# Feed-forward products transposed by the DMA crossbar in two planes of 16-bit halves instead of by TensorE

## The chip, the cores and the metric

One core of one Trainium2 chip runs the whole program. The metric is device time in microseconds of one execution, from the first to the last instruction and what lies around them; lower is better. Engines: PE (TensorE), PEld (its weight loads), DVE (VectorE), ACT (ScalarE), POOL (GpSimd), SP (SyncE, which here only issues transfers).

## What is computed

A decoder of four layers over 256 rows of 1024 values. Each layer is a token mixer (differential attention, stick-breaking attention, sliding-window attention, then differential attention again) and a feed-forward part, each between two RMS norms. The change touches the feed-forward part alone:

```python
def swiglu(h, w_gate, w_up, w_down):
    return (jax.nn.silu(h @ w_gate) * (h @ w_up)) @ w_down

x = x + rms_norm(m, norm_gains[i, 1])
f = swiglu(rms_norm(x, norm_gains[i, 2]), ffn_w_gate[i], ffn_w_up[i], ffn_w_down[i])
x = x + rms_norm(f, norm_gains[i, 3])
```

`w_gate` and `w_up` are 1024 x 2816, `w_down` is 2816 x 1024, all float32.

## The kernel before, in words

The 256 rows are two **streams** of 128 rows (s = 0 and 1). Both run the same program and share the weights. A **unit** of weights is a tile of 128 x 1024 float32 that SP fetches into a stage buffer (`load_dma`, four stage buffers); ACT then copies it, rounded, to `hi`, and DVE subtracts to get `lo` (`split`). Eleven units of `hi` and `lo` are held (RING). Every product is three matmuls in fp32r: data high part by `hi`, data high part by `lo`, data low part by `hi`.

The feed-forward part (`ffn`) goes over 11 chunks of 256 hidden columns. For a chunk, `project` runs 24 matmuls of 512 columns into the PSUM bank `mm_f` (one bank for each stream), from four units: 256 columns of gate and 256 of up. Then ACT takes the tanh of half the gate (`t`), DVE makes `t = (t + 1) * gate` and `h = t * hsq * up`, both of 128 x 256. `h` has the rows on the partitions; the product with `w_down` needs it the other way round. So PE transposes `h` in two blocks of 128 x 128 into a PSUM bank (`th_f`), and `split_rows` makes the high part `hTh` (ACT) and the low part `hTl` (DVE) from it. `down(c)` multiplies these with two units of `w_down` into two PSUM banks that gather over all chunks (`acc_f`), 12 matmuls of 512 columns for each chunk and stream. In chunk c the code runs `project(c)`, the instructions on `t` and `h`, `down(c - 1)`, and then the transposes of chunk c and `split_rows`; so `hTh` and `hTl` of chunk c are first used after `project(c + 1)`. Stream 1 runs about one chunk behind stream 0.

What sets the order: an `Emitter` writes the two streams and the weight splits out in one sequence, by a clock of its own (a matmul column counts 1/2.4 ns, a transposed column four times that), and every engine runs its instructions in the order in which they were written. An instruction that waits holds up all that stand behind it on its engine. SP's queue is also in order: the weight fetches stand in it, each waiting until its stage buffer is free.

The names in the profile leave buffer numbers out; where an instruction is issued through the helper that records engine calls, its line is L181. In the orders shown below `f104` is layer 1, stream 0, chunk 4, and `f113` layer 1, stream 1, chunk 3.

Of the kernel before, what the change touches and what calls it, by code (L numbers as in the profile page):

```python
# [9 lines left out]
F32 = mybir.dt.float32  # L10
F32R = mybir.dt.float32r
BF16 = mybir.dt.bfloat16
I32 = mybir.dt.int32
AF = mybir.ActivationFunctionType
ALU = mybir.AluOpType
AX = mybir.AxisListType
# [2 lines left out]
P = 128  # L19
# [5 lines left out]
NCH = HIDDEN // 256  # L25
# [8 lines left out]
TMP = 8  # L34
# [123 lines left out]
def trunk_kernel(ctx, tc, x, positions, norm_gains, a_w_in, a_w_out, a_lambda, a_subln, b_w_in, b_w_out,  # L158
                 c_w_in, c_w_out, c_sinks, w_gate, w_up, w_down, out, depth=DEPTH):
    nc = tc.nc  # L160
# [3 lines left out]
    wk = ctx.enter_context(tc.tile_pool(name="wk", bufs=2))  # L164
# [3 lines left out]
    def bank(tag, s, shape, name):  # L168
        return ps.tile(shape, F32, tag=f"{tag}{s}", name=name, bufs=BANKS[tag])
# [16 lines left out]
    act, dve, pool, pe = (Start(e) for e in (nc.scalar, nc.vector, nc.gpsimd, nc.tensor))  # L186
# [66 lines left out]
    def split(u):  # L253
        t = staged.pop(u)
        hi = ringp.tile([P, 1024], F32R, tag="hi", name=f"hi_{u}")
        lo = ringp.tile([P, 1024], F32R, tag="lo", name=f"lo_{u}")
        act.activation(hi, t, AF.Copy)
        dve.tensor_tensor(lo, t, hi.bitcast(F32), ALU.subtract)
# [10 lines left out]

    pos_i = sm.tile([P, 2], I32, name="pos_i", bufs=1)  # L270
    nc.scalar.dma_start(pos_i, positions.rearrange("b (s p) -> p (b s)", p=P))
# [17 lines left out]
    pool.memset(quarter, math.pi / 2)  # L289
    act.activation(sm.tile([P, 1], F32, tag="preload", name="preload", bufs=1), quarter, AF.Sin)  # L290
    for j in range(32):
# [25 lines left out]
    def tables():  # L317
# [22 lines left out]
        yield  # L340
        act.activation(c, r, AF.Abs)
        rv = r.rearrange("p (s n) -> p s n", s=2)
        cv = c.rearrange("p (s n) -> p s n", s=2)
        for h in range(2):
            act.activation(cosf[:, :, 32 * h:32 * h + 32], cv, AF.Sin, bias=quarter, scale=-1.0)
        act.activation(sinf[:, :, 0:32], rv, AF.Sin, scale=-1.0)
        act.activation(sinf[:, :, 32:64], rv, AF.Sin)

# [24 lines left out]
    def mm(o, a, b, start, stop, f32=False):  # L373
        pe.matmul(o, a, b, start=start, stop=stop)
        n = 1
        for d in o.shape[1:]:
            n *= d
        em.t += n * COLUMN_NS * (4 if f32 else 1)
# [6 lines left out]
    def transpose(o, i):  # L385
        pe.transpose(o, i, ident)
        em.t += P * COLUMN_NS * 4
# [81 lines left out]
    def rows_product(acc, ah, al, w, first, last):  # L469

        cols = [slice(h * 512, (h + 1) * 512) for h in range(2)]
        if last:
            for h, cs in enumerate(cols):
                mm3(acc[h], ah, al, w[0][:, cs], w[1][:, cs], first, last)
        else:
            for v in range(2):
                for h, cs in enumerate(cols):
                    mm(acc[h], ah, w[v][:, cs], first and v == 0, False)
            for h, cs in enumerate(cols):
                mm(acc[h], al, w[0][:, cs], False, False)  # L480
# [14 lines left out]
    def project(s, xn, n, units_, name, first):  # L495

        b = bank("acc" if first else "mm", s, [P, n], f"mm_{name}")
        per = KT // units_
        for u in range(units_):
            w = yield ("w",)  # L500
            js = [(per * u + j, slice(j * n, (j + 1) * n)) for j in range(per)]
            for kt, cs in js:
                for v in range(2):
                    mm(b, xn[0][:, kt, :], w[v][:, cs], kt == 0 and v == 0, False)
            for kt, cs in js:
                mm(b, xn[1][:, kt, :], w[0][:, cs], False, kt == KT - 1)
        return b
# [40 lines left out]
    def score_products(s, sc, q, k, mask):  # L548
# [6 lines left out]
        for j in range(2):  # L555
            kbs = [kb for kb in range(s + 1) if mask(kb) is not None]
            for kb in kbs:
                mm(sc[j][:, :, kb * P:(kb + 1) * P], identb, mask(kb).unsqueeze(1).to_broadcast([P, 2, P]), False, kb == kbs[-1])

    def two_groups(s, name):  # L560
        return [[wk.tile([P, 4, P], F32R, tag=f"o{p}{s}", name=f"o{p}_{name}{g}") for p in "hl"] for g in range(2)]

    def split_rows(oT, sl, src, scale=None):

        hi, lo = oT[0][:, sl, :], oT[1][:, sl, :]
        if scale is None:
            act.activation(hi, src, AF.Copy)
            dve.tensor_tensor(lo, src, hi.bitcast(F32), ALU.subtract)
        else:
            act.activation(hi, src, AF.Copy, scale=scale)  # L570
            dve.scalar_tensor_tensor(lo, src, scale, hi.bitcast(F32), ALU.mult, ALU.subtract)

    def layer_a(s, i, xn):
        inst = i // 3
        name = f"a{i}{s}"
        nk = s + 1
        tabs = scaled_tables(s, xn[2], name)
        oT = two_groups(s, name)
        wT, st, qT = {}, {}, {}

# [99 lines left out]
    def layer_b(s, i, xn):  # L680
        name = f"b{i}{s}"
        nk = s + 1
        n = nk * P
        oT = two_groups(s, name)
        aT, qT = {}, {}

# [87 lines left out]
    def layer_c(s, i, xn):  # L774
        name = f"c{i}{s}"
        nk = s + 1
        n = nk * P
        tabs = scaled_tables(s, xn[2], name)
        oT = two_groups(s, name)

        def keys(chunk):
# [76 lines left out]
    def ffn(s, i, xn):  # L858
        name = f"f{i}{s}"
        half = sm.tile([P, 1], F32, tag=f"half{s}", name=f"half_{name}", bufs=1)  # L860
        hsq = sm.tile([P, 1], F32, tag=f"hsq{s}", name=f"hsq_{name}", bufs=1)
        dve.tensor_scalar(half, xn[2], 0.5, None, ALU.mult)
        dve.tensor_tensor(hsq, half, xn[2], ALU.mult)
        acc = None
        hT = {}

        def down(c):
            nonlocal acc
            for j in range(2):
                w = yield ("w",)  # L870
                if acc is None:
                    acc = [bank("acc", s, [P, 512], f"acc_{name}_{q}") for q in range(2)]
                j2 = 2 * (c % 2) + j
                rows_product(acc, hT[c][0][:, j2, :], hT[c][1][:, j2, :], w, c == 0 and j == 0, c == NCH - 1 and j == 1)
            del hT[c]

        for c in range(NCH):
            chunk = yield from project(s, xn, 512, 4, f"{name}{c}", c == 0)
            t = wk.tile([P, 256], F32, tag=f"as{s}", name=f"t_{name}{c}", bufs=STEPS)
            h = wk.tile([P, 256], F32, tag=f"as{s}", name=f"h_{name}{c}", bufs=STEPS)  # L880
            act.activation(t, chunk[:, 0:256], AF.Tanh, scale=half)
            dve.scalar_tensor_tensor(t, t, 1.0, chunk[:, 0:256], ALU.add, ALU.mult)
            dve.scalar_tensor_tensor(h, t, hsq, chunk[:, 256:512], ALU.mult, ALU.mult)
            if c == NCH - 1:
                yield from down(c - 2)
                yield from down(c - 1)
            elif c in (0, NCH - 2):
                yield ("d", 2200)
            else:
                yield from down(c - 1)  # L890
            tp = bank("tp", s, [P, 2, P], f"th_{name}{c}")
            for j in range(2):
                transpose(tp[:, j, :], h[:, j * P:(j + 1) * P])
            if c % 2 == 0:
                hT[c] = hT[c + 1] = [wk.tile([P, 4, P], F32R, tag=f"o{q}{s}", name=f"hT{q}_{name}{c}") for q in "hl"]
            split_rows(hT[c], slice(2 * (c % 2), 2 * (c % 2) + 2), tp)
        yield ("d", 700)
        yield from down(NCH - 1)
        return acc

    def stream(s):
        if s:
            yield ("d", 1500)
        for i in range(depth):
            kind = i % 3
            xn = pre_norm(s, 4 * i, f"n{i}{s}")
            yield ("d", 600)
            if i == 0 and s:
                scalars()
                act.on = dve.on = pool.on = pe.on = False  # L910
            gain = gain_of(i, 1)
            oT, name = yield from (layer_a, layer_b, layer_c)[kind](s, i, xn)
            acc = yield from out_proj(s, oT, name, (1, 1, 3)[kind])
            post_norm(s, acc, gain, f"m{i}{s}")
            yield ("d", 4000)
            gain = gain_of(i, 3)
            xn = pre_norm(s, 4 * i + 2, f"q{i}{s}")
            yield ("d", 600)
            acc = yield from ffn(s, i, xn)
            post_norm(s, acc, gain, f"e{i}{s}")  # L920
            if i < depth - 1:
                yield ("d", 4000)
        for h in range(2):
            cs = slice(h * 512, (h + 1) * 512)
            nc.sync.dma_start(out[0, s * P:(s + 1) * P, cs], xs[s][:, cs])
# [27 lines left out]
```

## Time and profile before

| what | value |
|---|---|
| median of 3 runs | 1204.88 us (1204.61 to 1205.26) |
| the profiled execution | 1205.73 us |
| its span, first to last instruction | 1203.9 us |
| granted TensorE clock, mean | 0.998 of 2.4 GHz |
| PE busy | 1185.8 us, 98% of the span |
| DVE, ACT, POOL busy | 779.2, 656.9, 48.1 us |
| DMA | 205.90 MB, mean 171 GB/s |

All durations of the rows come from the profiled execution, which took 0.85 us more than the median and 1.8 us more than its own span. Busy time is the union of an engine's instructions; matmuls overlap each other, so the time that a matmul costs PE is read from the distance of starts, not from its duration.

### The profile page before, as it was taken

To read this page: it belongs to the slowest core of one execution; us is meant where nothing else is said; L and a number is where in the kernel's file an instruction comes from. 1 tells how busy PE (TensorE), PEld (TensorE's weight loads), DVE (VectorE), ACT (ScalarE), POOL (GpSimd) and SP (SyncE) were. 2 spreads that over 40 slices of the span, in tenths; PEclk is the share of its full clock that TensorE was granted. 3 is DMA by queue.
4 is the path that set the end of the run, shared out by engine and by line. 5 is a ranking of instruction groups with operands and counts; after the bars stand their busy time and mean duration, and the time that the engine had idled before them with its cause. 6 is when DMAs were issued, how large, how long until landed. Compare 5 with 4: busy or idle time off the path is not lost.

```text
span 1203.9 us, 16738 instructions
## 1 busy us (share of the span) xinstructions
PE 1185.8 (98%) x6028; PEld 971.6 (81%) x6028; DVE 779.2 (65%) x1217; ACT 656.9 (55%) x1197; POOL 48.1 (4%) x141
## 2 busy tenths in 40 slices
PE   8999999999999999999999999999999999999997
PEld 7787888888878888888888778888888788888886
DVE  7876765555847666555588666655587776655553
ACT  5665644444756665444476655444475565544442
POOL 2000100000200000000000000000010001000000
PEclk9999999999999999999999999999999999999999
DMA  8635465565644546656664246555565453566550
GB/s 280 206 120 159 151 192 186 189 192 179 225 139 123 176 140 193 191 181 189 192 199 135 88 144 191 191 189 187 185 205 156 129 175 123 179 189 192 180 170 35
DMA packets 140838, 205.90 MB, mean 171 GB/s; under 512 B 9554, under 2 KB 104916, under 8 KB 140756
## 3 DMA queue, kind: packets, MB, share of 16 engines
q1 hardware_dynamic: 140048, 204.51, 54.0%
q8 instruction: 47, 0.77, 0.3%
q10 hardware_dynamic: 708, 0.34, 0.1%
q14 instruction: 35, 0.29, 0.1%
HBM read 203.76 MB, written 1.05 MB: 170 GB/s over the span
## 4 chain that ended last, share of the span: by engine, by line
PE 90%; DVE 3%; ACT 3%; issue 2%; POOL 1%; DMA 1%; ACTq 0%; DVEq 0%; POOLq 0%
PE mm_f L181 39%; PE acc_f L181 18%; PE acc_a L181 3%; PE mm_c L181 2%; PE acc_b L181 2%; PE sc_a L181 2%; PE th_f L181 2%; DVE lo L181 1%; PE acc_c L181 1%; PE sc_b L181 1%; DMA stage<-in_a_w_in_dram 1%; ACT hi L181 1%; PE pv_a L181 1%; PE sc_c L181 1%; PE pv_c L181 1%
## 5 line engine op out<-in xcount | busy, mean ns | idle before, releaser
L181 DVE TENSOR_TENSOR lo<-stage,hi 128x1024 fp32r<-128x1024 f32 x378 | 461.0, 1223 | 285.5 <-ACT hi L181 283.6
L181 ACT ACTIVATE hi<-stage 128x1024 fp32r<-128x1024 f32 x378 | 399.5, 1061 | 324.1 <-PE mm_f L181 154.4
L181 PE MATMUL mm_f<-hi,xh_q 128*128 128x512 f32 x704 | 280.2, 398 | 0.0
L181 PE MATMUL mm_f<-lo,xh_q 128*128 128x512 f32 x704 | 274.5, 390 | 0.0
L181 PE MATMUL mm_f<-hi,xl_q 128*128 128x512 f32 x704 | 217.4, 390 | 1.0 <-DVE xl_q L181 1.0
L181 PEld LDWEIGHTS mm_f<-hi,xl_q 128*128 128x128 f32 x704 | 132.2, 188 | 30.4 <-DVE xl_q L181 1.9
L181 PEld LDWEIGHTS mm_f<-hi,xh_q 128*128 128x128 f32 x704 | 132.2, 188 | 26.1 <-ACT xh_q L181 0.2
L181 PEld LDWEIGHTS mm_f<-lo,xh_q 128*128 128x128 f32 x704 | 132.4, 188 | 25.8
L181 PE MATMUL acc_f<-hi,hTh_f 128*128 128x512 f32 x352 | 113.7, 399 | 0.5 <-ACT hTh_f L181 0.5
L181 PE MATMUL acc_f<-hi,hTl_f 128*128 128x512 f32 x352 | 111.4, 392 | 0.5 <-DVE hTl_f L181 0.4
L181 PE MATMUL acc_f<-lo,hTh_f 128*128 128x512 f32 x352 | 110.7, 390 | 0.0
L181 ACT ACTIVATE t_f<-mm_f,half_f 128x256 f32<-128x256 f32 x88 | 41.7, 474 | 79.7 <-PE mm_f L181 79.7
L181 PEld LDWEIGHTS acc_f<-hi,hTl_f 128*128 128x128 f32 x352 | 65.9, 188 | 14.9 <-DVE hTl_f L181 1.0
L181 PEld LDWEIGHTS acc_f<-lo,hTh_f 128*128 128x128 f32 x352 | 66.1, 188 | 14.0
L181 PEld LDWEIGHTS acc_f<-hi,hTh_f 128*128 128x128 f32 x352 | 63.7, 188 | 11.9 <-ACT hTh_f L181 0.8
L181 DVE SCALAR_TENSOR_TENSOR t_f<-t_f,mm_f 128x256 f32<-128x256 f32 x88 | 36.7, 417 | 35.2 <-ACT t_f L181 35.1
L181 DVE SCALAR_TENSOR_TENSOR h_f<-t_f,hsq_f,mm_f 128x256 f32<-128x256 f32 x88 | 42.3, 480 | 2.7
L181 ACT ACTIVATE hTh_f<-th_f 128x256 fp32r<-128x256 f32 x88 | 33.0, 375 | 17.0 <-PE th_f L181 16.7
L181 DVE TENSOR_TENSOR hTl_f<-th_f,hTh_f 128x256 fp32r<-128x256 f32 x88 | 36.5, 418 | 5.6 <-ACT hTh_f L181 5.3
L181 ACT ACTIVATE e_a<-sc_a,nm_a 128x128 f32<-128x128 f32 (+1 forms) x64 | 26.0, 420 | 17.1 <-DVE nm_a L181 16.9
L181 PE MATMUL th_f<-ident,h_f 128*128 128x128 f32 x176 | 33.5, 271 | 0.0
L181 PEld LDWEIGHTS th_f<-ident,h_f 128*128 128x128 f32 x176 | 24.1, 139 | 11.4 <-DVE h_f L181 0.3
(584 smaller groups left out, 1543.1 us busy)
## 6 DMA issues: line engine op xcount, KB each, us to landing
stage<-in_ffn_w_gate_dram SPq DMA_DIRECT2D x176, 256.0 KB, 2.9
stage<-in_ffn_w_up_dram SPq DMA_DIRECT2D x176, 256.0 KB, 3.1
stage<-in_ffn_w_down_dram SPq DMA_DIRECT2D x88, 512.0 KB, 3.5
stage<-in_a_w_in_dram SPq DMA_DIRECT2D x48, 512.0 KB, 3.8
stage<-in_b_w_in_dram SPq DMA_DIRECT2D x24, 512.0 KB, 3.6
stage<-in_a_w_out_dram SPq DMA_DIRECT2D x16, 512.0 KB, 3.9
stage<-in_c_w_in_dram SPq DMA_DIRECT2D x10, 512.0 KB, 3.6
gain<-in_norm_gains_dram SPq DMA_DIRECT2D x8, 512.0 KB, 4.1
```

Of the source, the lines that this page charges most:

```text
L181: i = call(*args, **kw)
```

## The change

For chunks 0 to 9 of every layer and stream (10 x 2 x 4 = 80 of 88 tiles `h`), `h` is taken as 16-bit words. POOL copies it into two planes, low words and high words (`hp`, 128 x 512 of uint16). One DMA transpose on SP's queue turns the four blocks of 128 x 128 (`hq`). POOL copies them back, interleaved, into a float32 tile (`hx`). `split_rows` reads `hx` from SBUF where it read `th_f` from PSUM. Chunk 10 keeps the two TensorE transposes.

```diff
+    def turned_by_dma(h, name):
+        planes = wk.tile([P, 2, 256], U16, tag="t2k", name=f"hp_{name}", bufs=TMP)
+        pool.tensor_copy(planes, h.bitcast(U16).rearrange("p (n w) -> p w n", w=2))
+        tq = wk.tile([P, 4, P], U16, tag="t2k", name=f"hq_{name}", bufs=TMP)
+        nc.sync.dma_start_transpose(tq, planes.rearrange("p w n -> p (w n)"))
+        t = wk.tile([P, 2, P], F32, tag="t2k", name=f"hx_{name}", bufs=TMP)
+        pool.tensor_copy(t.bitcast(U16).rearrange("p b (t w) -> p w b t", w=2), tq.rearrange("p (w b) t -> p w b t", w=2))
+        return t
...
-            tp = bank("tp", s, [P, 2, P], f"th_{name}{c}")
-            for j in range(2):
-                transpose(tp[:, j, :], h[:, j * P:(j + 1) * P])
+            if c == NCH - 1:
+                t = bank("tp", s, [P, 2, P], f"th_{name}{c}")
+                for j in range(2):
+                    transpose(t[:, j, :], h[:, j * P:(j + 1) * P])
+            else:
+                t = turned_by_dma(h, f"{name}{c}")
...
-            split_rows(hT[c], slice(2 * (c % 2), 2 * (c % 2) + 2), tp)
+            split_rows(hT[c], slice(2 * (c % 2), 2 * (c % 2) + 2), t)
```

Orders of one round in layer 1, without and with the change. First ACT, from the tanh of stream 0's chunk 4 to that of its chunk 5. Before:

```order
L181 ACTIVATE t_f104_4776<-mm_f104_4692,half_f10_4161 128x256
L181 ACTIVATE hi_159_4802<-stage_159_4738 128x1024
L181 ACTIVATE t_f113_4812<-mm_f113_4731,half_f11_4371 128x256
L181 ACTIVATE hi_160_4833<-stage_160_4757 128x1024
L181 ACTIVATE hTh_f104_4826<-th_f104_4823 128x256
L181 ACTIVATE hi_161_4852<-stage_161_4781 128x1024
L181 ACTIVATE hi_162_4877<-stage_162_4800 128x1024
L181 ACTIVATE hTh_f112_4727<-th_f113_4862 128x256
L181 ACTIVATE hi_163_4896<-stage_163_4831 128x1024
L181 ACTIVATE hi_164_4920<-stage_164_4849 128x1024
L181 ACTIVATE t_f105_4912<-mm_f105_4830,half_f10_4161 128x256
```

With the change:

```order
L182 ACTIVATE t_f104_4857<-mm_f104_4770,half_f10_4221 128x256
L182 ACTIVATE hi_159_4883<-stage_159_4819 128x1024
L182 ACTIVATE t_f113_4893<-mm_f113_4812,half_f11_4434 128x256
L182 ACTIVATE hi_160_4917<-stage_160_4838 128x1024
L182 ACTIVATE hTh_f104_4910<-hx_f104_4908 128x256
L182 ACTIVATE hi_161_4936<-stage_161_4862 128x1024
L182 ACTIVATE hTh_f112_4808<-hx_f113_4950 128x256
L182 ACTIVATE hi_162_4964<-stage_162_4881 128x1024
L182 ACTIVATE hi_163_4983<-stage_163_4915 128x1024
L182 ACTIVATE hi_164_5007<-stage_164_4933 128x1024
L182 ACTIVATE t_f105_4999<-mm_f105_4914,half_f10_4221 128x256
```

Both high parts now read `hx`, and stream 1's stands one weight split earlier, so that three splits follow it instead of two.

DVE in the same round, from stream 1's low part to the first weight split after stream 0's `h` of chunk 5. Before:

```order
L181 TENSOR_TENSOR hTl_f112_4728<-th_f113_4862,hTh_f112_4727 128x256
L181 TENSOR_TENSOR lo_163_4897<-stage_163_4831,hi_163_4896 128x1024
L181 TENSOR_TENSOR lo_164_4921<-stage_164_4849,hi_164_4920 128x1024
L181 SCALAR_TENSOR_TENSOR t_f105_4912<-t_f105_4912,mm_f105_4830 128x256
L181 SCALAR_TENSOR_TENSOR h_f105_4913<-t_f105_4912,hsq_f10_4162,mm_f105_4830 128x256
L181 TENSOR_TENSOR lo_165_4939<-stage_165_4874,hi_165_4938 128x1024
```

With the change:

```order
L182 TENSOR_TENSOR hTl_f112_4809<-hx_f113_4950,hTh_f112_4808 128x256
L182 TENSOR_TENSOR lo_162_4965<-stage_162_4881,hi_162_4964 128x1024
L182 TENSOR_TENSOR lo_163_4984<-stage_163_4915,hi_163_4983 128x1024
L182 TENSOR_TENSOR lo_164_5008<-stage_164_4933,hi_164_5007 128x1024
L182 SCALAR_TENSOR_TENSOR t_f105_4999<-t_f105_4999,mm_f105_4914 128x256
L182 SCALAR_TENSOR_TENSOR h_f105_5000<-t_f105_4999,hsq_f10_4222,mm_f105_4914 128x256
L182 TENSOR_TENSOR lo_165_5026<-stage_165_4961,hi_165_5025 128x1024
```

Between stream 1's low part and stream 0's next `h` there are three weight subtractions instead of two.

SP's queue and POOL with the change, in the same round (before, POOL has nothing there, and SP's queue is the same without the transposes). SP:

```order
L251 DMA stage_161_4862<-in_ffn_w_gate_dram 128x2x256
L251 DMA stage_161_4862<-in_ffn_w_up_dram 128x2x256
L247 DMA stage_162_4881<-in_ffn_w_down_dram 128x1024
L566 DMA_TRANSPOSE hq_f104_4906<-hp_f104_4904 128x4x128
L247 DMA stage_163_4915<-in_ffn_w_down_dram 128x1024
L566 DMA_TRANSPOSE hq_f113_4948<-hp_f113_4946 128x4x128
L251 DMA stage_164_4933<-in_ffn_w_gate_dram 128x2x256
L251 DMA stage_164_4933<-in_ffn_w_up_dram 128x2x256
```

POOL:

```order
L182 COPY hp_f104_4904<-h_f104_4858 128x512
L182 COPY hx_f104_4908<-hq_f104_4906 128x2x256
L182 COPY hp_f113_4946<-h_f113_4894 128x512
L182 COPY hx_f113_4950<-hq_f113_4948 128x2x256
L182 COPY hp_f105_5046<-h_f105_5000 128x512
L182 COPY hx_f105_5050<-hq_f105_5048 128x2x256
```

Every transpose stands right behind a fetch of `w_down` and ahead of the fetch of a later unit. On POOL the copy back of one stream stands ahead of the copy out of the other.

## Rows read from the trace of the kernel before

**Rows 1.** The page of the profiled execution: the busy time of each engine (part 1), the granted TensorE clock by slice (part 2), and the chain that ended last by engine and by line (part 4).

```profile
PE 1185.8 (98%) x6028; PEld 971.6 (81%) x6028; DVE 779.2 (65%) x1217; ACT 656.9 (55%) x1197; POOL 48.1 (4%) x141
...
PEclk9999999999999999999999999999999999999999
...
PE 90%; DVE 3%; ACT 3%; issue 2%; POOL 1%; DMA 1%; ACTq 0%; DVEq 0%; POOLq 0%
PE mm_f L181 39%; PE acc_f L181 18%; PE acc_a L181 3%; PE mm_c L181 2%; PE acc_b L181 2%; PE sc_a L181 2%; PE th_f L181 2%; DVE lo L181 1%; PE acc_c L181 1%; PE sc_b L181 1%; DMA stage<-in_a_w_in_dram 1%; ACT hi L181 1%; PE pv_a L181 1%; PE sc_c L181 1%; PE pv_c L181 1%
```

**Rows 2.** The windows view of one stretch inside the feed-forward part of the first and of the last layer. Columns: busy us and number of instructions of each engine, granted clock, busy share of the DMA engines, GB/s.

```profile
170.00:270.00 100.00, 100.00 (x452) 82.19 (x451) 57.23 (x72) 46.79 (x60) 0.00 (x0) 1.00 0.60 186
...
1050.00:1150.00 100.00, 100.00 (x451) 82.19 (x450) 58.34 (x72) 46.46 (x60) 0.00 (x0) 1.00 0.60 188
```

**Rows 3.** The timeline of ACT, and below it of DVE, over one round of the two streams in the first layer's feed-forward part. Columns: start us, us, engine, line, operation, out<-in, count, and in brackets the idle time before it and what ended it.

```profile
264.31 0.47 ACT L181 ACTIVATE t_f<-mm_f,half_f 128x256 f32<-128x256 f32 x1 [0.30 <-PE mm_f L181]
...
269.97 0.39 ACT L181 ACTIVATE hTh_f<-th_f 128x256 fp32r<-128x256 f32 x1 [0.16 <-PE th_f L181]
...
275.07 0.36 ACT L181 ACTIVATE hTh_f<-th_f 128x256 fp32r<-128x256 f32 x1
...
281.18 0.47 ACT L181 ACTIVATE t_f<-mm_f,half_f 128x256 f32<-128x256 f32 x1 [0.30 <-PE mm_f L181]
...
265.64 0.48 DVE L181 SCALAR_TENSOR_TENSOR h_f<-t_f,hsq_f,mm_f 128x256 f32<-128x256 f32 x1
266.76 1.23 DVE L181 TENSOR_TENSOR lo<-stage,hi 128x1024 fp32r<-128x1024 f32 x1 [0.64 <-ACT hi L181]
...
269.36 0.48 DVE L181 SCALAR_TENSOR_TENSOR h_f<-t_f,hsq_f,mm_f 128x256 f32<-128x256 f32 x1
269.85 1.23 DVE L181 TENSOR_TENSOR lo<-stage,hi 128x1024 fp32r<-128x1024 f32 x1
```

**Rows 4.** The timeline of PE round the second pair of transposes in the same round (columns as in Rows 3).

```profile
273.45 0.62 PE L181 MATMUL acc_f<-hi,hTl_f 128*128 128x512 f32 x2
273.91 0.38 PE L181 MATMUL th_f<-ident,h_f 128*128 128x128 f32 x2
274.04 0.48 PE L181 MATMUL mm_f<-hi,xh_q 128*128 128x512 f32 x1
274.36 0.40 PE L181 MATMUL mm_f<-lo,xh_q 128*128 128x512 f32 x1
```

**Rows 5.** Groups of instructions by line, engine, operation and shape: busy us, mean ns of one | idle before, and what ended most of it.

```profile
L181 DVE TENSOR_TENSOR lo<-stage,hi 128x1024 fp32r<-128x1024 f32 x378 | 461.0, 1223 | 285.5 <-ACT hi L181 283.6
L181 ACT ACTIVATE hi<-stage 128x1024 fp32r<-128x1024 f32 x378 | 399.5, 1061 | 324.1 <-PE mm_f L181 154.4 <-PE acc_f L181 92.2 <-PE acc_a L181 15.7
...
L181 DVE SCALAR_TENSOR_TENSOR h_f<-t_f,hsq_f,mm_f 128x256 f32<-128x256 f32 x88 | 42.3, 480 | 2.7
...
L181 DVE SCALAR_TENSOR_TENSOR t_f<-t_f,mm_f 128x256 f32<-128x256 f32 x88 | 36.7, 417 | 35.2 <-ACT t_f L181 35.1
...
L181 PE MATMUL th_f<-ident,h_f 128*128 128x128 f32 x176 | 33.5, 271 | 0.0
L181 ACT ACTIVATE hTh_f<-th_f 128x256 fp32r<-128x256 f32 x88 | 33.0, 375 | 17.0 <-PE th_f L181 16.7
```

**Rows 6.** The waits view: engine and instruction <- what it waited for: us in total, times, longest us. The first is ACT's largest wait ahead of a weight split, the second its largest for a weight transfer.

```profile
ACT hi L181 <- PE mm_f L181: 154.4, 121, 1.7
...
ACT hi L181 <- DMA stage<-in_a_w_in_dram: 6.4, 8, 1.9
```

**Rows 7.** The groups of POOL (columns as in Rows 5).

```profile
L181 POOL TENSOR_SCALAR u_e<-ssp_e 128x1 f32<-128x1 f32 x8 | 2.4, 301 | 668.5 <-ACT junk_e L181 668.5
...
L181 POOL TENSOR_TENSOR lprod<-lam_in 128x256 f32<-128x256 f32 x1 | 0.7, 740 | 0.0
L181 POOL MEMSET reset<- 128x256 f32 x1 | 0.3, 311 | 0.0
...
L181 POOL CAST identb<-ident 128x128 bf16<-128x128 f32 x1 | 0.3, 289 | 0.1
...
L181 POOL MEMSET mask_causal<- 128x128 bf16 x1 | 0.2, 204 | 0.0
```

**Rows 8.** The timeline of DVE, and below it of POOL, at the end of the first layer (columns as in Rows 3).

```profile
314.50 0.47 DVE L181 SCALAR_TENSOR_TENSOR h_f<-t_f,hsq_f,mm_f 128x256 f32<-128x256 f32 x1
314.89 3.49 DVE L181 TENSOR_TENSOR lo<-stage,hi 128x1024 fp32r<-128x1024 f32 x3
318.30 0.42 DVE L181 TENSOR_TENSOR hTl_f<-th_f,hTh_f 128x256 fp32r<-128x256 f32 x1
...
314.91 3.55 POOL L181 TENSOR_SCALAR u_n<-ss_n 128x1 f32<-128x1 f32 x1 [3.38 <-ACT junk_n L181]
```

**Rows 9.** DMA issues: queue, operation, count, KB of one, median us from issue to landing.

```profile
stage<-in_ffn_w_gate_dram SPq DMA_DIRECT2D x176, 256.0 KB, 2.9
...
stage<-in_ffn_w_down_dram SPq DMA_DIRECT2D x88, 512.0 KB, 3.5
...
out_dram<-x SPq DMA_DIRECT2D x4, 256.0 KB, 2.1
...
lam_in<-in_a_lambda_dram ACTq DMA_DIRECT2D x1, 256.0 KB, 5.0
...
nsink<-in_c_sinks_dram ACTq DMA_DIRECT2D x1, 8.0 KB, 5.5
```

More of the change, by code (lines that the diff above doesn't have):

```diff
@@ L13 @@
 I32 = mybir.dt.int32
+U16 = mybir.dt.uint16
 AF = mybir.ActivationFunctionType
```

## Prediction

> **What bounds the kernel now.** I read the page first. PE is busy 98% of the span and holds 90% of the chain that ended last, at a clock that stands at 2.4 GHz in all 40 slices [rows 1]. The windows view says the same of the feed-forward part alone: PE has no idle time there, DVE is busy 57 to 58% and ACT 46 to 47% [rows 2]. So a microsecond taken off PE is a microsecond gained, as long as the other engines keep up. On the chain the transposes `th_f` have 2% [rows 1].
>
> Next the timeline. One **round** (one chunk of each stream) lasts 281.18 - 264.31 = 16.87 us, the distance of two tanh of stream 0 [rows 3]. Within it ACT takes up `hTh` at 269.97 and 275.07, while DVE had `h` ready at 266.12 and 269.84: 3.85 and 5.23 us later [rows 3]. That delay is free now, because PE works on other things meanwhile. ACT mostly waits for PE ahead of a weight split (154.4 us), since all eleven weight buffers are full, and hardly for a transfer (6.4 us, and that in the mixer) [rows 6].
>
> **Removed.** PE loses 80 pairs of transposes of the 88 (160 of 176 instructions, [rows 5]). What a pair costs is read from starts: two `acc_f` start at 273.45 and, 0.23 later, 273.68; without the pair the two matmuls after it would start at 273.91 and 274.14. The second one starts at 274.36 [rows 4]: 0.22 to 0.23 us for a pair, taken as 0.23. 80 x 0.23 = **18.4 us**, all of it on the path. A round bounded by PE would last 16.87 - 2 x 0.23 = 16.41 us. (The group's 33.5 us busy counts overlap with neighbours, so it is not the price.)
>
> **Added, the way of one tile.** From the end of `h` to the start of `hTh` there is now a chain with the length L:
> - copy out on POOL, 512 columns. No such copy is in the trace. Lower end: the cast of 128 columns takes 289 ns, and a further column costs 0.83 ns by the two memsets, (311 - 204) / 128 [rows 7]: 0.29 + 384 x 0.83 ns = 0.61 us. Upper end: `lprod`, two inputs, takes 740 ns for 256 columns [rows 7], so 1.48 us. One input is nearer the cast: I take 0.7.
> - transpose on SP, issue to landing, 128 KB. Lower end 2.1 us, the write of `x` out of SBUF. Upper end 5.5 us, `nsink`, the slowest landing. `lam_in`, 256 KB in short pieces, takes 5.0, and the 512 KB fetch on the same queue 3.5 [rows 9]. I take 3.6, the middle of 2.1 and 5.0, next to that fetch.
> - copy back on POOL, the same bounds; it writes every second word: 0.8.
> - four handovers of some 0.05 us: 0.2. In the rows `lo` starts within 0.1 us of its `hi`, and POOL within 0.1 of ACT.
>
> L = 0.7 + 3.6 + 0.8 + 0.2 = **5.3 us** (3.5 to 8.7 by the ends).
>
> **Where L lies on the path.** POOL runs copy out and copy back of stream 0, then those of stream 1; so the two L of a round follow each other. ACT has `hTh` of stream 1 in its queue ahead of three weight splits, and DVE has its three `lo` ahead of the `t` and `h` of stream 0's next chunk, which starts the next L (the orders shown with the change). This closes a loop: L, L, `hTh` 0.38, one `hi` 1.06, three `lo` 3 x 1.22 = 3.67, `t` 0.42, `h` 0.48 [rows 5], and 0.1 for handovers: 2L + 6.1. The other two splits and the tanh on ACT are done by then (0.38 + 3 x 1.06 + 0.47 = 4.03, before the last `lo` ends at 5.1).
>
> **The lock between DVE and POOL.** At 314.91 POOL starts an instruction `u_n` on one column; it takes 3.55 us and ends 0.08 after the third of three `lo` that DVE runs back to back from 314.89 to 318.38. The like of it, `u_e`, takes 0.30 [rows 7, 8]. So POOL cannot read beside a `lo`, which reads two tiles from SBUF, and gets no turn between two of them. In the changed order a `lo` stands right behind `h`, its `hi` is ready by then, and a `lo` starts within 0.02 us of the end of `h` (269.84 to 269.85, [rows 3]). So the copy out of stream 0 comes behind one `lo`: **1.2 us** more in each round. Stream 1's copy out starts when POOL comes free, while DVE waits for `hTh`: nothing. The Trainium skill (SBUF — State Buffer, section SBUF: two separate sides) states it as an exclusive lock between a VectorE instruction with two SBUF inputs and a GpSimd one that reads SBUF, held for the whole instruction by whichever starts first; the trace agrees with its 3.55 us. Were the copy first, DVE would wait instead.
>
> **The sum.** A round lasts 2 x 5.3 + 6.1 + 1.2 = 17.9 us, more than the 16.41 of PE, so the loop bounds it: +1.03 us against 16.87. There are 10 chunks x 4 layers = 40 rounds: +41 us. The profiled execution took 1205.7, so 1247; the median of the runs is 0.85 lower, so **1246 us**.
>
> **Costed at nothing.** SP's queue: each transpose holds back the fetches behind it until POOL has copied, and adds its own issue. The cover is the full weight buffers [rows 6]; ACT needs the unit behind stream 1's transpose only after that stream's `hTh` and two more splits, when a fetch (2.9 to 3.5 us, [rows 9]) has had the transpose, the copy back and 2.1 us. If that cover is gone, `hi` is late next, on the same loop. DMA engines: 60% busy in these stretches [rows 2], so a transpose may queue behind a fetch; that is inside 2.1 to 5.5. The split now reads SBUF, off PE's path. The buffers of the new tiles come round after 8 of them, over two tiles `h`. PE's idle time in a round is 17.9 - 16.4 = 1.5 us; no row shows the clock fall, so none is charged.
>
> **Rivals.**
> 1. *The crossbar is quick, PE stays the bound: faster.* The point is 2L + 7.3 = 16.87, L = 4.79, a transpose of 3.1 us with the copies as taken; below 2.9 nothing of the loop is seen. At the low ends, L = 3.5 gives 14.3, under 16.41, and the time is 1205.7 - 18.4 = 1187 us. For it speak the 2.1 and 2.9 us of plain transfers of twice the bytes; against it, that a transpose moves 2-byte words and stands behind a 512 KB fetch in SP's queue. If the lock alone does not bite, the round is 16.7 and the time 1199. The Trainium skill (Advanced Engine Details and Errata, section X-Bar Transpose (TRN2)) says that such transposes are as fast as regular transfers; no row here shows one, and by that rule this rival wins.
> 2. *The crossbar is slow.* At the 5.0 of `lam_in`, L = 6.7, the round is 20.7 and the time 1205.7 + 3.83 x 40 = 1359 us; at all the upper ends (L = 8.7, round 24.7) it is 1519. For it speaks that short pieces land latest [rows 9]; against it, that those two landed on another queue at the start. The Trainium skill (VectorE: DVE Perf Modes, section The three transpose paths) gives 1309 ns for one 128 x 128 block through the crossbar against 390 on TensorE, and advises TensorE where the result may go to PSUM, as here; no run here shows it. As an estimate by that page, four blocks one after another are 5.2 us, which would be this rival. Within it lies a clock that falls because PE idles (every round would then need twice PE's 16.4); 0.02.
> 3. *Even.* A loop within 0.06 us of the old round.
>
> That the transposes are not replaced can be left out: PE has 80 pairs fewer in its order.
>
> **How the numbers follow.** About 0.2% (2.4 us) is what a measurement of this kernel can tell from no change. The forecast, 1208 to 1300 us (a transpose of 3.1 to 4.3 us with the copies as taken), has 0.47. Rival 1 has 0.23, rival 3 0.05, rival 2 (over 1300) 0.25, about half of it over 1370. The range goes from the floor of PE, 1186, to 1370, which a transpose of 5.1 us gives. Cases of both signs lie in it; the forecast's own range is 1208 to 1300. Faster 0.23, same 0.05, slower 0.72.
>
> **What would show it.** Right: rounds of 17 to 20 us by the distance of stream 0's tanh; `hTh` on ACT waiting for POOL, 80 times; `hp` stretched by about 1.2 us in one stream; PE idle some 1.5 us in a round. Each term has its row: copies 0.7 and 0.8, landing 3.6. Wrong: PE without idle time and rounds of 16.4 (rival 1), or landings over 4.5 us (rival 2), or waits of `hi` for a fetch, which would make SP's queue the cause.

## The result and the profile after

Before 1204.89 us in the median of four runs (1204.61 to 1205.26); after **1190.55 us** (1187.64 to 1192.48). The profiled run of the changed kernel took 1192.19 us, with a span of 1190.4. The change makes the kernel faster, by 1.2%: ratio 0.9879, interval [0.986, 0.9897]. The four runs after lie 4.8 us apart, those before 0.7; that spread is part of what has to be explained. From here, lines of the changed kernel are one higher than before (L182 for L181).

The page of the changed kernel: busy times, the chain that ended last, groups (busy us, mean ns of one | idle before, and what ended it) and DMA issues (KB, median us from issue to landing).

```profile
PE 1168.0 (98%) x5868; PEld 958.5 (81%) x5868; DVE 779.4 (65%) x1217; ACT 649.0 (55%) x1197; POOL 175.0 (15%) x301
...
PE 68%; DMA 10%; DVE 7%; POOL 5%; ACT 5%; issue 4%; SPq 0%; POOLq 0%; ACTq 0%; DVEq 0%
...
L182 ACT ACTIVATE hTh_f<-hx_f 128x256 fp32r<-128x256 f32 x80 | 33.4, 418 | 229.4 <-POOL hx_f L182 229.4
...
L182 POOL COPY hp_f<-h_f 128x512 uint16<-128x512 uint16 x80 | 70.4, 880 | 301.5 <-DVE h_f L182 273.0
...
L182 POOL COPY hx_f<-hq_f 128x512 uint16<-128x512 uint16 x80 | 62.8, 785 | 254.8 <-DMA hq_f<-hp_f 252.5
...
stage<-in_ffn_w_gate_dram SPq DMA_DIRECT2D x176, 256.0 KB, 3.1
...
stage<-in_ffn_w_down_dram SPq DMA_DIRECT2D x88, 512.0 KB, 4.5
...
hq_f<-hp_f SPq DMA_TRANSPOSE x80, 2.5
```

Against [rows 1] the share of PE in the chain fell from 90% to 68%, that of DMA rose from 1 to 10% and that of POOL from 1 to 5%: the loop that the prediction described exists, and PE is no longer the only bound. `hTh` waits for the copy back all 80 times, 229.4 us. The median landing is 2.5 us from issue, and the fetches land later than in [rows 9] (3.1 for 2.9, 4.5 for 3.5).

The windows view, one stretch of the first and one of the last layer:

```profile
170.00:270.00 100.00, 100.00 (x443) 82.81 (x442) 57.52 (x72) 45.25 (x61) 21.77 (x26) 1.00 0.77 210
...
1050.00:1150.00 100.00, 97.33 (x420) 79.14 (x419) 57.08 (x72) 45.16 (x60) 20.99 (x24) 0.98 0.72 202
```

PE has no idle time in the first stretch, as in [rows 2], but 2.67 us in the second. By the distance of stream 0's tanh a round lasts 16.3 us where PE bounds it: in layers 1 and 2 all six rounds that begin with chunks 3 to 8 of stream 0. In layer 0 single rounds take 16.5 to 17.2, in layer 3 16.7 to 18.1. Two tanh of stream 0 in layer 1, then two in layer 3:

```profile
526.09 0.47 ACT L182 ACTIVATE t_f<-mm_f,half_f 128x256 f32<-128x256 f32 x1 [0.30 <-PE mm_f L182]
542.41 0.47 ACT L182 ACTIVATE t_f<-mm_f,half_f 128x256 f32<-128x256 f32 x1 [0.30 <-PE mm_f L182]
```

```profile
1091.65 0.45 ACT L182 ACTIVATE t_f<-mm_f,half_f 128x256 f32<-128x256 f32 x1
1109.78 0.45 ACT L182 ACTIVATE t_f<-mm_f,half_f 128x256 f32<-128x256 f32 x1
```

In layer 1 the tanh waits for PE and the round is 16.32 us; in layer 3 it waits for nothing but its place in ACT's order, and the round is 18.13. A late round does not always cost what it is late: in layer 0 shorter ones, down to 15.3 us, follow, and the stretch from the first tanh to the last takes 173.99 us, against 173.44 in the kernel without transposes (first experiment). In layer 3 it takes 178.82 against 173.44. So the gain is the predicted floor of PE, less what the late rounds cost, which in the profiled execution is nearly all in layer 3.

POOL's timeline over the latest round, in layer 3, shows the loop whole (start us, us, what, and in brackets the idle time before and what ended it):

```profile
1094.38 1.45 POOL L182 COPY hp_f<-h_f 128x512 uint16<-128x512 uint16 x1 [5.93 <-DVE h_f L182]
1101.93 0.76 POOL L182 COPY hx_f<-hq_f 128x512 uint16<-128x512 uint16 x1 [6.10 <-DMA hq_f<-hp_f]
1102.60 0.61 POOL L182 COPY hp_f<-h_f 128x512 uint16<-128x512 uint16 x1
1105.82 0.77 POOL L182 COPY hx_f<-hq_f 128x512 uint16<-128x512 uint16 x1 [2.60 <-DMA hq_f<-hp_f]
1112.51 1.45 POOL L182 COPY hp_f<-h_f 128x512 uint16<-128x512 uint16 x1 [5.93 <-ACT t_f L182]
```

Copy out and back of stream 0, copy out and back of stream 1, then 5.93 us in which ACT and DVE do the splits, the tanh and the next `h`. The 5.93 recurs to 0.02 us in every round of layers 0 and 3 that begins with chunks 2 to 8, as read from POOL's timeline there. (In the sums of the loop, here and below, the landing of a turn is POOL's idle time between copy out and copy back.) With 1.45 for the first copy, 0.76, 0.61, 2.56 for the usual landing of stream 1, 0.76 and 5.93, less 0.08 by which the records overlap, the loop is **12.0 us + landing of stream 0**. The landings of layer 0 and 3 check it: 4.67 gave a round of 16.68, 5.21 gave 17.20, 6.10 gave 18.13. By this sum a round is over PE's 16.3 when that landing is over 4.3 us. In the 12 rounds of layers 0 and 3 that begin with chunks 3 to 8, all of them set by the loop, the landings of stream 0 run from 3.34 to 6.10, median 4.2: the loop stands at the balance with PE. Six of these rounds are late: four have a landing of stream 0 over 4.3, and in the other two, of 16.5 and 17.5 us, stream 1's landing took 3.12 and 4.15.

DVE beside the first of these rows, in the same kernel, shows why that copy takes 1.45 us and not 0.61:

```profile
1093.74 0.48 DVE L182 SCALAR_TENSOR_TENSOR h_f<-t_f,hsq_f,mm_f 128x256 f32<-128x256 f32 x1
1094.14 1.22 DVE L182 TENSOR_TENSOR lo<-stage,hi 128x1024 fp32r<-128x1024 f32 x1
```

The copy starts 0.24 us into a `lo` and ends 0.47 after it. In layers 1 and 2 this `lo` comes later, because its `hi` waits there for PE to free a weight buffer, and the copy takes 0.61. With that and landings of 4.2 us in the median (3.56 to 4.76) the same sum is 15.3 us in these layers, and PE sets the round.

### The profile page after: what moved, and what is told of

Same layout as the page of the kernel before. It is cut to its first block, busy times and chain, and to the rows that moved or that the text cites. A ratio compares the mean times of both kernels' runs of the same rounds, so it can differ in the third digit from the quotient of the medians.

```text
span 1190.4 us, 16818 instructions
## 1 busy us (share of the span) xinstructions
PE 1168.0 (98%) x5868; PEld 958.5 (81%) x5868; DVE 779.4 (65%) x1217; ACT 649.0 (55%) x1197; POOL 175.0 (15%) x301
## 4 chain that ended last, share of the span: by engine, by line
PE 68%; DMA 10%; DVE 7%; POOL 5%; ACT 5%; issue 4%; SPq 0%; POOLq 0%; ACTq 0%; DVEq 0%
PE mm_f L182 26%; PE acc_f L182 12%; DMA hq_f<-hp_f 8%; DVE lo L182 4%; PE acc_a L182 3%; POOL hp_f L182 3%; ACT hi L182 2%; PE mm_c L182 2%; PE acc_b L182 2%; PE sc_a L182 2%; POOL hx_f L182 1%; PE acc_c L182 1%; DMA stage<-in_a_w_in_dram 1%; PE sc_b L182 1%; PE pv_a L182 1%
## 5 line engine op out<-in xcount | busy, mean ns | idle before, releaser
L182 DVE TENSOR_TENSOR lo<-stage,hi 128x1024 fp32r<-128x1024 f32 x378 | 457.6, 1224 | 130.3 <-ACT hi L182 127.6
L182 ACT ACTIVATE hi<-stage 128x1024 fp32r<-128x1024 f32 x378 | 393.8, 1056 | 124.9 <-PE mm_f L182 49.9
L182 PE MATMUL mm_f<-hi,xh_q 128*128 128x512 f32 x704 | 275.8, 392 | 2.3 <-DVE h_f L182 2.3
L182 PE MATMUL mm_f<-lo,xh_q 128*128 128x512 f32 x704 | 274.8, 390 | 0.0
L182 PE MATMUL mm_f<-hi,xl_q 128*128 128x512 f32 x704 | 217.5, 390 | 1.0 <-DVE xl_q L182 1.0
L182 ACT ACTIVATE hTh_f<-hx_f 128x256 fp32r<-128x256 f32 x80 | 33.4, 418 | 229.4 <-POOL hx_f L182 229.4
L182 PEld LDWEIGHTS mm_f<-hi,xh_q 128*128 128x128 f32 x704 | 132.6, 188 | 30.9 <-ACT t_f L182 2.4
L182 PEld LDWEIGHTS mm_f<-hi,xl_q 128*128 128x128 f32 x704 | 132.4, 188 | 29.5 <-DVE xl_q L182 1.8
L182 PEld LDWEIGHTS mm_f<-lo,xh_q 128*128 128x128 f32 x704 | 132.6, 188 | 27.4 <-DVE lo L182 0.2
L182 DVE TENSOR_TENSOR hTl_f<-hx_f,hTh_f 128x256 fp32r<-128x256 f32 x80 | 34.0, 425 | 162.9 <-ACT hTh_f L182 162.9
L182 POOL COPY hp_f<-h_f 128x512 uint16<-128x512 uint16 x80 | 70.4, 880 | 301.5 <-DVE h_f L182 273.0
L182 PE MATMUL acc_f<-hi,hTh_f 128*128 128x512 f32 x352 | 111.3, 392 | 0.5 <-ACT hTh_f L182 0.5
L182 PE MATMUL acc_f<-lo,hTh_f 128*128 128x512 f32 x352 | 110.6, 390 | 0.7 <-DVE lo L182 0.5
L182 PE MATMUL acc_f<-hi,hTl_f 128*128 128x512 f32 x352 | 111.0, 391 | 0.0
L182 POOL COPY hx_f<-hq_f 128x512 uint16<-128x512 uint16 x80 | 62.8, 785 | 254.8 <-DMA hq_f<-hp_f 252.5
L182 PEld LDWEIGHTS acc_f<-lo,hTh_f 128*128 128x128 f32 x352 | 65.9, 188 | 15.2 <-DVE lo L182 1.5
L182 PEld LDWEIGHTS acc_f<-hi,hTh_f 128*128 128x128 f32 x352 | 65.7, 188 | 14.3 <-ACT hTh_f L182 0.8
L182 PEld LDWEIGHTS acc_f<-hi,hTl_f 128*128 128x128 f32 x352 | 65.8, 188 | 14.0 <-DVE hTl_f L182 0.5
L182 ACT ACTIVATE t_f<-mm_f,half_f 128x256 f32<-128x256 f32 x88 | 41.3, 469 | 59.6 <-PE mm_f L182 59.3
L182 DVE SCALAR_TENSOR_TENSOR t_f<-t_f,mm_f 128x256 f32<-128x256 f32 x88 | 36.6, 416 | 20.5 <-ACT t_f L182 20.4
L182 DVE SCALAR_TENSOR_TENSOR h_f<-t_f,hsq_f,mm_f 128x256 f32<-128x256 f32 x88 | 42.3, 480 | 2.9
L182 ACT ACTIVATE e_a<-sc_a,nm_a 128x128 f32<-128x128 f32 (+1 forms) x64 | 26.0, 420 | 17.0 <-DVE nm_a L182 16.9
```

The costliest lines, as they stand in the source:

```text
L182: i = call(*args, **kw)
```

## Experiments

The kernel before ran beside them at 1205.7 us (first four), 1205.2 (the next three) and 1205.15 (the last).

### The floor: no transposes at all

In place of the transposes `h` itself is handed to the split; the transposes of ten chunks are left out.

```
-                t = turned_by_dma(h, f"{name}{c}")
+                t = h.rearrange("p (b t) -> p b t", b=2)
```

> Leaves the transposes of chunks 0 to 9 out altogether: the split reads h as it is (the products with w_down then use an h that is not turned). No hp, hq, hx; PE's order is that of the changed kernel. Theory (PE is the bound, the way through the crossbar is nearly hidden): the floor of the prediction, 1204.9 - 80 x 0.23 = 1186.5 us, rounds of 16.3 to 16.4 us in all four layers, and a spread of the runs as small as before (under 1 us); the 4 us by which the changed kernel lies above that are late transposes. Rival (the gain or the rest comes from the changed order, not from the transposes): about 1190.5 with the same uneven rounds in layers 0 and 3.

Measured: 1185.17 us (1184.95 to 1185.64), ratio 0.9831 [0.9817, 0.9844], rounds of 16.3 in all layers. The floor holds; the changed kernel stands 5.4 us above it (6.2 when each is set against the kernel before that ran beside it). The windows give the share of the DMA engines without the transposes:

```profile
170.00:270.00 100.00, 100.00 (x443) 82.81 (x442) 59.66 (x73) 48.15 (x61) 0.00 (x0) 1.00 0.62 194
```

0.62, against 0.77 after: some 13 transposes in 100 us take 15% of all 16 engines, although they move 1.7 MB beside 19. The page counts their packets, first in the changed kernel, then in this one:

```profile
DMA packets 184361, 216.42 MB, mean 182 GB/s; under 512 B 53074, under 2 KB 148436, under 8 KB 184276
```

```profile
DMA packets 140837, 205.88 MB, mean 174 GB/s; under 512 B 9555, under 2 KB 104917, under 8 KB 140757
```

That is 544 more small packets for each of the 80 transposes, of some 240 bytes.

### The transposes on ScalarE's queue

```
-        nc.sync.dma_start_transpose(tq, planes.rearrange("p w n -> p (w n)"))
+        nc.scalar.dma_start_transpose(tq, planes.rearrange("p w n -> p (w n)"))
```

> The DMA transposes are issued from ACT's queue instead of SP's. Theory (the landings over 2.5 us, up to 6, come from standing behind weight fetches in SP's queue): all 80 landings near 2.5 us, rounds of 16.3 us in all layers, 1187 to 1188 us. Rival (the DMA engines are shared, whichever queue a transfer stands in): landings from 2.5 to 6 us as now, 1190 to 1192 us. Against both: ACT now issues 1.2 us for each transpose and waits for POOL ahead of stream 1's tanh; if that binds, rounds are longer everywhere and the time is over 1195.

Measured: 1274.85 us (1272.53 to 1275.07), ratio 1.057 [1.0555, 1.0584]. The landings did not become shorter: from chunk 3 on stream 0's transposes took 4.9 to 7.3 us, the median of all is 3.7. So it isn't the place in SP's queue that delays them. What goes with a late landing, on either queue, is the fetches under way: in the changed kernel's trace, of the 71 transposes whose landing is recorded, the 50 issued with at most 512 KB of fetches not yet landed took 2.4 us in the median, the 21 issued with more (768 KB or 1 MB) took 4.0; here the 31 with more, up to 1.5 MB, took 5.3. And ACT, in order, now stands behind each transpose's copy out and its issue of 1.2 us (waits view):

```profile
ACT hi L182 <- issue: 57.9, 32, 3.1
ACT t_f L182 <- issue: 45.8, 11, 4.7
```

### Each transpose twice

The first of the two writes a tile that nobody reads.

```
+        nc.sync.dma_start_transpose(wk.tile([P, 4, P], U16, tag="t2k", name=f"hd_{name}", bufs=TMP), planes.rearrange("p w n -> p (w n)"))
         nc.sync.dma_start_transpose(tq, planes.rearrange("p w n -> p (w n)"))
```

> Every DMA transpose is issued twice in a row from SP's queue, the first into a tile that nobody reads; the copy back waits for the second. L grows by one issue, 1.2 us: 0.61 + 2.5 + 1.2 + 0.76 + 0.2 = 5.3 us. Theory (the loop of the prediction is right and only its landing time was mis-sized): a round is 2 x 5.3 + 6.1 + 0.84 (the lock as the copy out shows it) = 17.5 us instead of 16.3, so 1190.5 + 40 x 1.2 = 1238 us. Rival (the way through the crossbar is off the path, with buffers enough to hide it): 1190 to 1195 us, rounds of 16.3 us.

Measured: 1262.18 us (1260.18 to 1264.65), ratio 1.047 [1.0456, 1.0484]. Nothing was added for PE, and 72 us came: the turn is on the loop. The median of the 24 rounds that begin with chunks 3 to 8 is 18.1 us, and the part of the loop on ACT and DVE is 5.83 or 5.84 in all 24, so PE sets none of them. The loop closes again: stream 1's turn takes 3.87 instead of 2.56 (the issue of the other transpose ahead of it), stream 0's copy 1.54, its turn 4.78 in the median: 1.54 + 4.78 + 0.76 + 0.61 + 3.87 + 0.76 + 5.84 - 0.09 = 18.07. The expected time was 24 us short, 0.6 us a round, above all because it took 3.7 us (2.5 + 1.2) for stream 0's turn, which took 4.78.

### One stream only

```
-            if c == NCH - 1:
+            if c == NCH - 1 or s == 1:
```

> Only stream 0's tiles go through the crossbar, stream 1 keeps the TensorE transposes. PE saves half, 40 x 0.23 = 9.2 us. Theory (two ways in a row make a tile late): with one way in each round nothing is late, 1204.9 - 9.2 = 1195.7 us with a spread under 1 us. Rival (each tile is late by itself, because of fetches on the same queue): half the excess stays too, 1197.5 to 1198.5 us, and the runs spread over 2 us or more.

Measured: 1196.23 us (1195.97 to 1196.45), ratio 0.9922 [0.9909, 0.9934], rounds of 16.6. With one turn in the loop instead of two PE sets every round, with landings of 2.4 to 5.1, and the pair of transposes that stays in a round costs PE 16.57 - 16.32 = 0.25 us, close to the 0.23 of [rows 4].

### Both copies out ahead of both copies back

The changed kernel's POOL order lets the second turn begin only after the first has come back. Here the copy back and the split are written one stage of the next chunk later. On POOL, out, back, out, back becomes out, out, back, back; the other engines' orders stay.

```
     def turned_by_dma(h, name):
...
         nc.sync.dma_start_transpose(tq, planes.rearrange("p w n -> p (w n)"))
+        return tq
+
+    def joined(tq, name):
...
+            if u == 1 and late is not None:
+                late()
...
-            split_rows(hT[c], slice(2 * (c % 2), 2 * (c % 2) + 2), t)
+                late = lambda d=hT[c], sl=sl, t=t, n=f"{name}{c}": split_rows(d, sl, joined(t, n))
```

> The copy back (hx) and the split of a chunk's transpose are written one stage of the next chunk later, so that GpSimd's order becomes copy out of stream 0, copy out of stream 1, copy back of stream 0, copy back of stream 1, where the changed kernel has out, back, out, back. The order on TensorE, VectorE, ScalarE and SyncE is unchanged. Theory (what the changed kernel still pays above the 1185.2 us of the kernel without transposes is its loop, in which the two streams' turns stand one behind the other on GpSimd): the two landings now overlap, the loop of a round is 5.9 + copy out 1.45 + landing 3.3 + two copies back 1.5 + 0.2 = 12.4 us, and 16.3 is reached only with a landing of over 7 us: 1185 to 1186.5 us, rounds of 16.3 in all four layers, spread of the runs under 1 us. Rival (the late landings and the fetches that they hold up cost the time whatever GpSimd's order): 1189 to 1192 with the same spread of some 5 us.

Measured: 1186.26 us (1185.81 to 1186.81), ratio 0.9843 [0.9828, 0.9858], rounds of 16.3 in all four layers, spread 1.0 us. Its windows:

```profile
1050.00:1150.00 100.00, 100.00 (x443) 82.81 (x442) 60.84 (x74) 47.32 (x62) 24.85 (x25) 1.00 0.74 207
```

PE's idle time in the last layer is gone, at the same DMA share, although landings still reach 6.0 us. So 4.3 of the 5.4 us above the floor were the loop, not the transfers as such. The chain that ended last is PE's again, and the wait of `hTh` for the copy back is still there:

```profile
PE 87%; DVE 4%; ACT 3%; DMA 2%; issue 2%; POOL 2%; POOLq 0%; ACTq 0%; DVEq 0%; SPq 0%
```

```profile
ACT hTh_f L182 <- POOL hx_f L182: 190.4, 80, 4.6
```

So 80 waits do not by themselves show that the loop binds; the chain and the length of the rounds do.

### The same, each transpose twice

> As the kernel with the pairs on GpSimd, and each transpose is issued twice, the first into a tile that nobody reads (160 crossbar transposes instead of 80). Theory (the loop alone): the pairs leave some 4 us a round, and the two extra transposes take at most 2 x 2.5 us of them: rounds of 16.3 to 17.4, 1186 to 1200 us, against 1262 for the doubled transposes with the old order on GpSimd. Rival (the bytes and small packets of the crossbar themselves slow the fetches and so TensorE): no better than 1240.

Measured: 1218.05 us (1211.68 to 1221.9), ratio 1.0117 [1.0093, 1.0141]. Between the two theories: against 1262.18 with the old order, 44 of the 72 us are gone, and 32 over 1186.26 stay, where at most 14 were expected. Its windows, its waits, and below them the same wait of the changed kernel:

```profile
170.00:270.00 100.00, 98.69 (x431) 80.34 (x430) 57.98 (x73) 44.49 (x59) 27.36 (x25) 1.00 0.88 220
```

```profile
ACT hi L182 <- DMA stage<-in_ffn_w_up_dram: 45.7, 36, 2.7
```

```profile
ACT hi L182 <- DMA stage<-in_ffn_w_up_dram: 4.7, 8, 0.9
```

The DMA engines are at 0.88, and the splits now wait 45.7 us for weights (4.7 in the changed kernel, none in the feed-forward part with the pairs and single transposes). This points to the DMA engines as a second bound when the transposes are doubled; no run tests it alone. How the 32 us divide between these waits and what is left of the loop stays open.

### The splits later, POOL's order as changed

```
+            with tc.issue_after(last["hi"].ins):
+                act.activation(hi, t, AF.Copy)
+            with tc.issue_after(last["lo"].ins):
+                dve.tensor_tensor(lo, t, hi.bitcast(F32), ALU.subtract)
```

`last` holds the newest weight split at that point.

> GpSimd's order is that of the changed kernel (out, back, out, back); instead the splits are moved: on ScalarE and VectorE stream 0's hTh and hTl stand one weight split (hi, lo) later, and stream 1's two later, so that only one weight split instead of three stands between stream 1's hTl and the next tanh of stream 0. Theory: two lo of 1.22 us leave the loop, 15.3 - 2.4 = 12.9 us with a landing of 3.3, and 16.3 is reached with a landing of 6.7: 1185 to 1187 us. Rival (the landings cost the time whatever the order): 1189 to 1192.

Measured: 1186.26 us (1185.74 to 1187.33), ratio 0.9844 [0.9829, 0.9859], rounds of 16.3 (one of 16.4). `hTh` waits for the copy back 28 times and 49.2 us, where it was 80 times and 229.4:

```profile
ACT hTh_f L182 <- POOL hx_f L182: 49.2, 28, 3.6
```

Two different edits that shorten the loop, at another place each, give the same time. Both versions beat the changed kernel and the one before.

### Without the lock on stream 0's copy out

```
+            planes = planes_of(h, f"{name}{c}", dve) if s == 0 and c < NCH - 1 else None
...
+                t = turned_by_dma(planes or planes_of(h, f"{name}{c}", pool), f"{name}{c}")
```

> Only stream 0's copy out (hp) moves: VectorE makes it right behind h, ahead of the weight split's lo, instead of GpSimd beside that lo. GpSimd still has copy back of stream 0, copy out and copy back of stream 1 in this order, so the two turns of a round still follow each other. In the changed kernel this copy takes 0.61 us in layers 1 and 2 and 1.45 to 1.66 beside a lo in layers 0 and 3; the loop of a late round there is 1.45 + landing + 0.76 + 0.61 + 2.56 + 0.76 + 5.93 = 12.07 us + landing of stream 0. Theory (the lock on the copy out decides which rounds are late): with some 0.4 to 0.6 us for the copy on VectorE the loop is 11.0 to 11.2 + landing, and only a landing of over 5.1 us makes a round later than PE's 16.3, which 5 of 40 rounds had: 1185.5 to 1187.5 us, spread under 2 us. Rival (the lock only takes up slack; late landings make the late rounds): 1189 to 1192 us with a spread of some 5 us.

Measured: 1190.49 us (1189.2 to 1192.84), ratio 0.9884 [0.9867, 0.99]. The theory fell, the rival held: the copy takes 0.43 us on DVE, and the time is that of the changed kernel. SP's queue in the first layer suggests why. First the changed kernel, one round, the last fetch ahead of stream 0's transpose (here of `up`, with two more pairs of gate and up ahead of it; 61 of the 80 transposes stand behind a fetch of `w_down`), and POOL's copy back:

```profile
263.59 0.47 SPq L251 DMA_DIRECT2D stage<-in_ffn_w_up_dram  x1
265.63 1.20 SPq L566 DMA_TRANSPOSE hq_f<-hp_f  x1
```

```profile
268.94 0.76 POOL L182 COPY hx_f<-hq_f 128x512 uint16<-128x512 uint16 x1 [3.34 <-DMA hq_f<-hp_f]
```

Then the kernel with the copy on DVE:

```profile
263.17 0.46 SPq L251 DMA_DIRECT2D stage<-in_ffn_w_up_dram  x1
264.07 1.19 SPq L570 DMA_TRANSPOSE hq_f<-hp_f  x1
```

```profile
269.13 0.77 POOL L182 COPY hx_f<-hq_f 128x512 uint16<-128x512 uint16 x1 [11.33 <-DMA hq_f<-hp_f]
```

Counted from the issue of the last fetch, the transpose is issued after 0.9 us instead of 2.0 and the copy back starts after 6.0 instead of 5.4: issued 1.1 us earlier, it lands no earlier. In the rounds set by the loop the copy and the landing together have a median of 5.7 us in the changed kernel (12 rounds) and 6.0 here (17). Three `lo` back to back free three stage buffers within 2.3 us, and 1.5 MB of fetches go out just ahead of stream 0's transpose. Both instants fit a transpose that comes in when those have drained: with over 512 KB under way the median landing is 4.8 us here, 4.0 in the changed kernel. No run took the fetches away, so this cause is not shown by an experiment. What is shown is that without the lock the transpose starts earlier and does not land earlier.

## Why the prediction was wrong, point by point

- **PE's gain** held. 80 pairs were 18.4 us on paper; the kernel without transposes is 20.5 us faster than the one beside it. The floor of 1186.5 by the median was 1185.2, rounds of 16.41 were 16.32.
- **The loop and its order** held: the POOL rows above show every member in the place that was predicted, the chain of the changed kernel runs through it, and both edits that shorten the loop brought the time to within 1.1 us of the floor.
- **The step that failed is the price of the loop**, 17.9 us, where layers 0 and 3 show 16.2 and layers 1 and 2 15.3. The largest wrong term is "transpose, issue to landing: 3.6 us", taken for both turns of a round. Stream 1's landing is 2.56 (1.04 less), with few fetches ahead of it; stream 0's is 4.2 in the median of the 12 rounds set by the loop (0.6 more). One value for two places with different traffic was the mistake: the 512 KB fetch and `lam_in` of [rows 9], which drew the value up to the middle of 2.1 and 5.0, bound a transpose behind other transfers, and `out<-x`, 2.1 us, one with free engines.
- **The small terms** are together larger than what is left of the landing's error (1.04 less 0.6), and all lean one way. The copies are 0.61 and 0.76 for 0.7 and 0.8 (0.26 less for the four). The lock made 0.84 of 1.2 in layers 0 and 3, since the copy starts inside the `lo`, and nothing in layers 1 and 2, where the step "its `hi` is ready by then" failed. The part from `hTh` on, with the handovers and the overlap of the records, is 5.85 for 6.1 + 0.4 (0.65 less).
- **The sum** for layers 0 and 3 therefore: 17.9 - 1.04 + 0.6 - 0.26 - 0.36 - 0.65 = 16.2 us, all but PE's own round of 16.3, where the prediction had 1.5 more than PE. **Rival 1 came nearest**: PE bounds layers 1 and 2, and its 1187 us lies 3.5 below the median, the late rounds. It was to decide at L = 4.79; L is 3.9 for stream 1 and 5.6 for stream 0, without the lock, 4.75 in the mean. So by the prediction's own 2L + 7.3 the right L alone would have given 16.8 us for these layers, even with the old round. The gain needed the 7.3 to be wrong too: it measured 5.85 + 0.84 = 6.7.
- **The lock** is there (0.61 us alone, 1.45 beside a `lo`); that agrees with the Trainium skill (SBUF — State Buffer, section SBUF: two separate sides). But removing it changed nothing: stream 0's copy, lock and landing were priced at 5.5 us and took 5.65, and without the lock the landing grew. As a charge of its own beside the landing it was counted twice.
- **The page that spoke against the change**, the Trainium skill (VectorE: DVE Perf Modes, section The three transpose paths), has 1309 ns for one block, from which the prediction made an estimate of 5.2 us for four; here one transpose of 128 x 512 two-byte words, four blocks, lands in 2.5 us when little is ahead of it. The rule of the Trainium skill (Advanced Engine Details and Errata, section X-Bar Transpose (TRN2)), as fast as a regular transfer, is nearer: 2.5 us stands between the 2.1 and 2.9 of plain transfers of 256 KB [rows 9], though this one is 128 KB.
- **Costed at nothing**: the cover of SP's queue held (`hi` waits for a fetch of `up` 4.7 us in all, 8 times). That a transpose may queue behind a fetch "inside 2.1 to 5.5" was the right place and was then not followed: the late rounds are those with a late landing, up to 6.1 us.
- **The spread** was not foreseen. With the loop at the balance with PE, a landing 1 us later makes a round 1 us later, and the order of times with the late `lo` in layers 1 and 2 has 0.84 us more room than that of layers 0 and 3. The kernels with a shorter loop spread by 1.0 and 1.6 us, which fits; each kernel has one trace, so it is not shown which rounds differ between runs.

## What to carry to other kernels

When a sum stands within 10% of the bound, each of its terms can decide the sign, so price a transfer at each place where it is issued, by what goes out on the same engines in the microseconds ahead of it, and not once for all. When work moves from the bound engine onto a chain through other engines, ask first whether two such chains can run beside each other: here the order of four copies on an idle engine was worth 4 us. An earlier start of a transfer gained nothing here; price it by what is still under way when it is issued. And a wait that recurs in every round shows a bound only if the chain runs through it.

## What the runs showed of the hardware

- A transpose of 128 x 512 two-byte words through the crossbar holds its issuing queue for 1.2 us, on SP and on ACT alike, and lands in 2.4 to 2.5 us with little under way. With 768 KB or 1 MB of fetches under way it took 2.8 to 5.9 us from SP's queue, with 768 KB to 1.5 MB 3.7 to 7.3 from ACT's.
- A copy out of 512 two-byte words that takes 0.61 us on POOL takes 0.43 on DVE.
- Once, PE stood idle for 2.0 us ahead of 1145.57, in the changed kernel's last layer. The granted clock then stood at 0.50, the 1.2 GHz level, before it came back. The matmul that ended the idle time, and the windows view:

```profile
1145.57 0.56 PE L182 MATMUL mm_f<-hi,xh_q 128*128 128x512 f32 x1 [2.01 <-DVE h_f L182]
```

```profile
1143.60:1145.50 1.90, 0.00 (x0) 0.00 (x0) 1.86 (x4) 1.08 (x2) 0.00 (x0) 1.00 0.68 263
1145.80:1149.20 3.40, 3.40 (x9) 2.64 (x9) 2.71 (x4) 1.06 (x1) 1.23 (x1) 0.50 0.82 289
```

Matmuls started every 0.43 us there, against 0.23 in [rows 4]: an estimate from these starts is 1.7 us, beside the 2.0 idle, of the 6.6 us by which this execution's span exceeds that of the kernel without transposes (1190.4 and 1183.8). The kernels whose rounds were late throughout had this more often, nine times in the one with each transpose twice and five in the one on ACT's queue, start and end of the program aside. The prediction had charged nothing for it, as no row of the feed-forward part showed it.
